# Hybrid SSD and S5 encoder layer on one core: the decayed scores go through PSUM, their differences go to ScalarE, and the norm weights are applied to four feature tiles at once

## The chip, the cores and the metric

The kernel runs on one core of one Trainium2 chip. The metric is the device time of one execution in microseconds (us), median of several runs. Every product is made in fp32r with a split operand: a value is stored as a rounded high part and a low remainder, and one product is three matmuls (high by high, high by low, low by high).

## What is computed

A layer over 2048 tokens (16 more are put ahead and dropped again), width 1024. Only the parts that matter here are shown.

```python
xn = rmsnorm(h, norm_mix_w)
z, xbc, dt_raw, u_s5, gates = split(xn @ w_in)
y_a = ssd_branch(z, xbc, dt_raw, ...)
y_b = s5_branch(u_s5, ...)
h = h + (g_a * y_a + g_b * y_b) @ w_out
h = h + square(relu(rmsnorm(h, norm_mlp_w) @ w_ff_in)) @ w_ff_out
return rmsnorm(h, final_norm_w)[16:]
...
def ssd_chunked(xs, dt, a, bm, cm):
    da_cs = cumsum(dt_c * a)
    seg = da_cs[:, :, :, None] - da_cs[:, :, None, :]
    decay = exp(where(causal, seg, -inf))
    scores = einsum("bclgn,bcsgn->bclsg", cc, bc)
    y_diag = einsum("bclsg,bclsgr,bcsgrp->bclgrp", scores, decay, xdt)
    states = einsum("bclgn,bclgr,bclgrp->bcgrpn", bc, decay_states, xdt)
    ...
    y_off = einsum("bclgn,bcgrpn,bclgr->bclgrp", cc, h_prev, exp(da_cs))
    return y_diag + y_off
```

The SSD branch has 16 heads of width 64 in 4 groups; the heads of a group share bm and cm (128 states).

## The kernel before

The work has three stages. An **initial stage** normalises all rows and makes the S5 inputs from them, while tables for S5 are set up on VectorE. Then four **mixer blocks** (b = 0 to 3) of 512 tokens follow. Last comes the **MLP**, in three row blocks; the change does not touch it.

The norm of a row tile (128 rows) is `norm_rows`: `scale_rows` multiplies 128x1024 values by a scalar of each row, `turn_rows` then transposes the eight feature tiles on TensorE into two PSUM banks of four and writes them out as high and low part with the norm weight of each feature. It runs for 16 row tiles and the 16 extra rows in the initial stage, and again for 12 row tiles (blocks 1 to 3) at the end of the block before.

A mixer block takes the groups g = 0 to 3 in turn. For a group, four tiles of the convolution's input (two of xs, one of b, one of c) and then 16 products for z and the gate run on TensorE. They are the dense work: tiles named `pd`, in four PSUM banks of their own. The SSD work rides along: after each of the group's eight weight units `step` is called, with `t` from 0 to 7, and issues some of it. It uses four other PSUM banks, which `bank` hands out in turn: a new tile waits until the tile that was four before it has been read for the last time.

Of a chunk of 128 tokens (`c` = 0 to 3), `inputs` and `front` transpose xs into the bank `sst` (L787), multiply it by dt (`xdt`, L791) and by the skip weight (`dx`, L830), make the scores in the bank `psc` (three matmuls, issued by `mm3`), mask them (`smask`, L837), multiply the decays of four heads by them (L839) and split the result (`mh` on ScalarE, L842, `ml` on VectorE, L843). `back` makes y: the part from the state (`pyo`), and for each of four heads one matmul of `mh` with both halves of `xhl` side by side (L853) and one of `ml` with the high half (L855). VectorE then adds the two halves to y one after the other (L864). `update` brings the state `hT` forward (`pS`); the next chunk's `pyo` needs it.

The decays of a group come from `decays`: a DMA on SP's queue (L885) spreads the cumulative sums `csd` over all partitions (1 MB, tile `csb`), VectorE subtracts the sum of each partition and takes the minimum with 0 (16 instructions of 128x128, L889), and ScalarE takes the exponential in place (L890). `start` is called at t = 2; `csb` has one buffer in block 0 and two in the others. `csd` of a block is written by its first step.

In block 0 the S5 recurrence also rides along (`s5.step`), with long runs of VectorE work. In what order the instructions stand on an engine is set by a scheduler when the program is built: it simulates the program and places an instruction where it thinks it ready, after the points that `tc.issue_after` names. Once built, each engine works strictly in that order.

Of the kernel before, what the change touches and what calls it, by code (L numbers as in the profile page):

```python
# [9 lines left out]
F32 = mybir.dt.float32  # L10
F32R = mybir.dt.float32r
AF = mybir.ActivationFunctionType
ALU = mybir.AluOpType
# [3 lines left out]
P = 128  # L17
# [8 lines left out]
NG = 4  # L26
# [101 lines left out]
def _body(ctx, tc, d, out):  # L128
    nc = tc.nc
    V, S, G, T = nc.vector, nc.scalar, nc.gpsimd, nc.tensor  # L130
# [14 lines left out]
    def bank(name, dt=F32):  # L145
        return pss.tile([P, 512], dt, name=name, tag="s")
# [7 lines left out]
    tri = cm.tile([P, P], F32, name="tri")  # L154
# [86 lines left out]
    def mm3(ps, lh, ll, rh, rl, first, last, open_=False):  # L241


        T.matmul(ps, lh, rh, start=first, stop=False, skip_group_check=open_)  # L244
        T.matmul(ps, lh, rl, start=False, stop=False, skip_group_check=open_)  # L245
        return T.matmul(ps, ll, rh, start=False, stop=last, skip_group_check=open_).ins  # L246
# [12 lines left out]

    def scale_rows(pl, src, L, rs):  # L260
        t = pl.tile([P, D], F32, name="nt", tag="nt", bufs=2)
        V.tensor_scalar(t[:L], src[:L], rs, None, op0=ALU.mult)
        return t

    def norm_rows(pl, src, L, rs, wcol, dh, dl, c0):
# [2 lines left out]
    def turn_rows(t, L, wcol, dh, dl, c0, qs=(0, 1)):  # L268
        for q in qs:
            p = bank("ntp")  # L270
            pv = p.rearrange("p (f l) -> p f l", f=4)[:, :, :L]
            for i in range(4):
                ft = q * 4 + i
                T.transpose(pv[:, i, :], t[:L, ft * P:(ft + 1) * P], ident[:L, :L])
            for i in range(4):
                ft = q * 4 + i
                S.activation(dh[:, ft, c0:c0 + L], pv[:, i, :], AF.Copy, scale=wcol[:, ft:ft + 1])
                V.scalar_tensor_tensor(dl[:, ft, c0:c0 + L], pv[:, i, :], wcol[:, ft:ft + 1],
                                       dh[:, ft, c0:c0 + L].bitcast(F32), op0=ALU.mult, op1=ALU.subtract)


    def s5_setup(stack):
# [493 lines left out]
    class Ssd:  # L776
# [5 lines left out]

        def inputs(self, x, dts, i0, cs_, L):
            pl = self.pl
            pt = bank("sst")
            for i in range(2):
                T.transpose(pt[:L, i * P:(i + 1) * P], self.sd.xs[:, i, cs_], ident)  # L787
            x.pth = pt[:L, 0:256].rearrange("p (h q) -> p h q", h=4)
            x.xdt = pl.tile([P, 4, 64], F32, name="xdt", tag="xdt")
            xdd = pl.tile([P, 4, 64], F32, name="xdd", tag="xdd")  # L790
            V.tensor_tensor(x.xdt[:L], x.pth, h4(dts.dt, L, i0), op=ALU.mult)  # L791
            G.tensor_tensor(xdd[:L], x.xdt[:L], h4(dts.ds, L, i0), op=ALU.mult)
            x.xddh = pl.tile([P, 256], F32R, name="xddh", tag="xddh", bufs=2)
            x.xddl = pl.tile([P, 256], F32R, name="xddl", tag="xddl", bufs=2)
            xf = xdd.rearrange("p h q -> p (h q)")
            S.copy(x.xddh[:L], xf[:L])
            G.tensor_tensor(x.xddl[:L], xf[:L], x.xddh[:L].bitcast(F32), op=ALU.subtract)
# [14 lines left out]
            G.tensor_tensor(self.hl, f, self.hh.bitcast(F32), op=ALU.subtract)  # L812

        def start(self):
            self.dec = decays(self.pl, self.dts, self.g, self.b)

        def meta_in(self):
            self.mk = _K()
# [5 lines left out]
        def front(self, c):  # L824

            pl, sd, g, x = self.pl, self.sd, self.g, self.ck[c]
            x.cs_ = cs_ = slice(sd.t0 + c * P, sd.t0 + (c + 1) * P)
            self.inputs(x, self.dts, c * NH + g * 4, cs_, P)
            x.dx = pl.tile([P, 4, 64], F32, name="dx", tag="dx", bufs=2)
            V.tensor_tensor(x.dx, x.pth, drow[:, g * 4:g * 4 + 4].unsqueeze(2).broadcast_to([P, 4, 64]), op=ALU.mult)  # L830
            x.xhl = pl.tile([P, 4, 2, 64], F32R, name="xhl", tag="xhl", bufs=2)
            S.copy(x.xhl[:, :, 0, :], x.xdt)
            G.tensor_tensor(x.xhl[:, :, 1, :], x.xdt, x.xhl[:, :, 0, :].bitcast(F32), op=ALU.subtract)
            psc = bank("psc")
            mm3(psc[:, 0:P], sd.bh[:, cs_], sd.bl[:, cs_], sd.ch[:, cs_], sd.cl[:, cs_], True, True)
            sm = pl.tile([P, P], F32, name="smask", tag="smask", bufs=2)
            V.tensor_tensor(sm, psc[:, 0:P], tri, op=ALU.mult)  # L837
            csb = self.dec[:, c]
            V.tensor_tensor(csb, csb, sm.unsqueeze(1).broadcast_to([P, 4, P]), op=ALU.mult)  # L839
            x.mh = pl.tile([P, 4, P], F32R, name="mh", tag="mh", bufs=2)  # L840
            x.ml = pl.tile([P, 4, P], F32R, name="ml", tag="ml", bufs=2)
            S.copy(x.mh, csb)  # L842
            V.tensor_tensor(x.ml, csb, x.mh.bitcast(F32), op=ALU.subtract)  # L843

        def back(self, c):

            pl, sd, g, x, dts = self.pl, self.sd, self.g, self.ck[c], self.dts
            i0, cs_ = c * NH + g * 4, x.cs_
            py, po = bank("py"), bank("pyo")
            mm3(po[:, 0:256], sd.ch[:, cs_], sd.cl[:, cs_], self.hh, self.hl, True, True)  # L850
            pyv = py.rearrange("p (h a q) -> p h a q", h=4, a=2)
            for h in range(4):
                T.matmul(pyv[:, h].rearrange("p a q -> p (a q)"), x.mh[:, h, :],  # L853
                         x.xhl[:, h].rearrange("p a q -> p (a q)"), start=True, stop=False)
                T.matmul(pyv[:, h, 0, :], x.ml[:, h, :], x.xhl[:, h, 0, :], start=False, stop=True)  # L855
            self.update(x, sd.bth[:, c, :], sd.btl[:, c, :], dts.cd, i0, P)
            if c < NC4 - 1:
                self.split()
            x.y = y = pl.tile([P, 4, 64], F32, name="y_", tag="y_", bufs=2)
            for h in range(4):  # L860
                V.scalar_tensor_tensor(y[:, h, :], po[:, h * 64:h * 64 + 64], dts.E[:, i0 + h:i0 + h + 1],
                                       x.dx[:, h, :], op0=ALU.mult, op1=ALU.add)
            for a in range(2):
                V.tensor_tensor(y, y, pyv[:, :, a, :], op=ALU.add)  # L864

        def gate(self, c):

# [13 lines left out]
    def decays(pl, dts, g, b):  # L881

        t = pl.tile([P, NC4, 4, P], F32, name="csb", tag="csb", bufs=2 if b else 1)
        src = csd[b].rearrange("(c h) l -> c h l", h=NH)[:, g * 4:g * 4 + 4, :]
        nc.sync.dma_start(t, src.unsqueeze(0).broadcast_to([P, NC4, 4, P]))  # L885
        for c in range(NC4):
            for h in range(4):
                i = c * NH + g * 4 + h
                V.tensor_scalar(t[:, c, h, :], t[:, c, h, :], dts.cs[:, i:i + 1], 0.0, op0=ALU.subtract, op1=ALU.min)  # L889
        S.activation(t, t, AF.Exp)  # L890
        return t


    xp = pool("xn", stack=xp_st)
# [195 lines left out]
    for b in range(NB):  # L1090
# [10 lines left out]
        ssd, later = {}, []  # L1101
# [11 lines left out]
        def step(mm):  # L1113

            n = step.n
            step.n += 1
            g, t = divmod(n, 8)
            with tc.issue_after(mm):
                if n == 0:
                    dts.turn()  # L1120
                    dts.sums()
                if g < NG:
                    x = ssd[g]
                    if t == 2:
                        x.start()
                    elif t == 4:
                        if b == 0:
                            x.meta_in()
                        x.front(0)
                    elif t == 5:  # L1130
                        if b == 0:
                            x.meta_out()
                        x.split()
                        x.front(1)
                    elif t == 6:
                        x.back(0)
                    elif t == 7:
                        x.front(2)
                        x.gate(0)
                if g > 0:  # L1140
                    x = ssd[g - 1]
                    if t == 0:
                        x.back(1)
                        x.gate(1)
                    elif t == 1:
                        x.front(3)
                    elif t == 2:
                        x.back(2)
                        x.gate(2)
                    elif t == 3:  # L1150
                        x.back(3)
                        x.gate(3)
                for f in later:
                    f()
                later.clear()
                if b == 0:
                    s5.step(n - 1)
                if n >= KSTART:
                    next(kept, None)
# [79 lines left out]
        for c in range(NC4):  # L1239
# [4 lines left out]
            p = bank("y5p")  # L1244
# [521 lines left out]
```

## Time and profile before

| | |
|---|---|
| median of 3 runs | 3305.94 us (3300.7 to 3306.1) |
| the profiled execution | 3306.5 us, of which 3304.8 us are the span from the first to the last instruction |
| TensorE busy | 3083.7 us, 93% |
| VectorE busy | 2105.5 us, 64% |
| ScalarE busy | 1231.2 us, 37% |
| GpSimd busy | 1428.1 us, 43% |

A group of instructions is named by its line, its engine (PE is TensorE, DVE VectorE, ACT ScalarE, POOL GpSimd, SP the queue of SyncE), and its tiles as out<-in. A busy time counts stretches in which an engine had an instruction in flight; successive instructions overlap a little, so that the busy time of a group divided by their number is less than the mean duration. An engine's idle time matters only where another engine waits for it.

### The profile page before, as it was taken

To read this page: it belongs to the slowest core of one execution; us is meant where nothing else is said; L and a number is where in the kernel's file an instruction comes from. 1 tells how busy PE (TensorE), PEld (TensorE's weight loads), DVE (VectorE), ACT (ScalarE), POOL (GpSimd) and SP (SyncE) were. 2 spreads that over 40 slices of the span, in tenths; PEclk is the share of its full clock that TensorE was granted. 3 is DMA by queue.
4 is the path that set the end of the run, shared out by engine and by line. 5 is a ranking of instruction groups with operands and counts; after the bars stand their busy time and mean duration, and the time that the engine had idled before them with its cause. 6 is when DMAs were issued, how large, how long until landed. Compare 5 with 4: busy or idle time off the path is not lost. (4 is left out here: it accounts for less than half of the span.)

```text
span 3304.8 us, 50038 instructions
## 1 busy us (share of the span) xinstructions
PE 3083.7 (93%) x18353; PEld 2751.1 (83%) x18353; DVE 2105.5 (64%) x4298; ACT 1231.2 (37%) x2573; POOL 1428.1 (43%) x1736
## 2 busy tenths in 40 slices
PE   7899999998999999998999788998979999989998
PEld 6678888877888778876888688888979999989998
DVE  8969998426843576426854477767675555475555
ACT  6345554434432443334433343344442121142222
POOL 3346766523522344213433465665642222243443
PEclk9999999999999999999999889999989999999999
DMA  6477676775556654566756767777788888889998
GB/s 210 143 214 203 199 205 205 284 245 155 173 189 216 201 169 158 204 221 195 226 178 209 255 252 275 261 275 265 276 283 284 246 250 245 249 286 377 358 358 277
DMA packets 297877, 782.92 MB, mean 237 GB/s; under 512 B 90688, under 2 KB 132800, under 8 KB 268448
## 3 DMA queue, kind: packets, MB, share of 16 engines
q0 software_dynamic: 88832, 411.21, 37.4%
q1 hardware_dynamic: 206192, 367.29, 33.8%
q8 instruction: 146, 2.39, 0.3%
q10 hardware_dynamic: 2608, 1.22, 0.1%
q14 instruction: 99, 0.81, 0.1%
HBM read 563.66 MB, written 218.05 MB: 237 GB/s over the span
## 5 line engine op out<-in xcount | busy, mean ns | idle before, releaser
L1505 DVE TENSOR_TENSOR acc<-acc,p 128x512 f32<-128x512 f32 x330 | 225.7, 684 | 171.6 <-PE p L246 169.1
L244 PE MATMUL pd<-hnh,wc 128*128 128x384 f32 (+1 forms) x896 | 292.9, 328 | 34.9 <-DMA wc<-wcd 21.3
L244 PE MATMUL pd<-wu,xnh 128*128 128x512 f32 x768 | 309.8, 404 | 3.5 <-ACT cacc L750 3.0
L246 PE MATMUL pd<-wu,xnl 128*128 128x512 f32 x768 | 308.9, 402 | 0.0
L245 PE MATMUL pd<-wu,xnh 128*128 128x512 f32 x768 | 308.3, 401 | 0.0
L246 PE MATMUL pd<-hnh,wc 128*128 128x384 f32 (+1 forms) x896 | 291.6, 328 | 13.7 <-DVE wc L1346 10.5
L245 PE MATMUL pd<-hnl,wc 128*128 128x384 f32 (+1 forms) x896 | 291.8, 326 | 0.0
L228 POOL DMA_DIRECT2D wu<-wsd x168 | 96.0, 572 | 373.0 <-PE pd L246 305.6
L1356 POOL DMA_DIRECT2D wr<-wcd x227 | 122.3, 539 | 274.8 <-PE pd L246 138.7
L244 PE MATMUL pd<-xnh,wu 128*128 128x512 f32 (+1 forms) x640 | 232.8, 364 | 7.7 <-DMA wu<-wsd 6.5
L246 PE MATMUL pd<-xnh,wu 128*128 128x512 f32 (+1 forms) x640 | 229.3, 359 | 0.0
L245 PE MATMUL pd<-xnl,wu 128*128 128x512 f32 (+1 forms) x640 | 229.0, 358 | 0.0
L1356 POOL DMA_DIRECT2D wc<-wcd x221 | 118.3, 536 | 252.8 <-PE pd L246 136.8
L244 PEld LDWEIGHTS pd<-hnh,wc 128*128 128x128 f32 x896 | 173.6, 194 | 40.0 <-ACT hnh L994 13.5
L753 DVE SCALAR_TENSOR_TENSOR cacc<-craw,conv,cacc 128x512 f32<-128x512 f32 (+1 forms) x192 | 174.9, 912 | 24.5 <-ACT cacc L750 17.1
L246 PEld LDWEIGHTS pd<-hnh,wc 128*128 128x128 f32 x896 | 173.6, 194 | 19.9 <-DVE wc L1346 14.3
L244 PEld LDWEIGHTS pd<-wu,xnh 128*128 128x128 f32 x768 | 146.1, 190 | 35.4 <-ACT cacc L750 3.9
L245 PEld LDWEIGHTS pd<-hnl,wc 128*128 128x128 f32 x896 | 173.7, 194 | 0.0
L246 PEld LDWEIGHTS pd<-wu,xnl 128*128 128x128 f32 x768 | 146.3, 191 | 31.8 <-issue 0.2
L245 PEld LDWEIGHTS pd<-wu,xnh 128*128 128x128 f32 x768 | 146.0, 190 | 31.4 <-issue 0.2
L218 POOL TENSOR_TENSOR wu<-wst,wu 128x1024 fp32r<-128x1024 f32 x56 | 137.1, 2448 | 73.6 <-ACT wu L217 72.5
L244 PEld LDWEIGHTS pd<-xnh,wu 128*128 128x128 f32 x640 | 125.5, 196 | 24.9 <-issue 7.9
(1015 smaller groups left out, 9967.7 us busy)
## 6 DMA issues: line engine op xcount, KB each, us to landing
wu<-wsd POOLq DMA_DIRECT2D x168, 1024.0 KB, 5.3
wr<-wcd POOLq DMA_DIRECT2D x227, 512.0 KB, 5.1
wcd<-wc SPq DMA_DIRECT2D x224, 512.0 KB, 3.0
wc<-wcd POOLq DMA_DIRECT2D x221, 512.0 KB, 5.5
wsd<-wu SPq DMA_DIRECT2D x56, 1024.0 KB, 5.2
wst<-in_w SPq DMA_DIRECT2D x60, 512.0 KB, 5.8
csb<-csd SPq DMA_DIRECT2D x16, 1024.0 KB, 14.3
xt<-in_x SPq DMA_DIRECT2D x28, 512.0 KB, 3.8
```

What stands on the lines that cost most here:

```text
L218: eng.tensor_tensor(t[:, 1], raw, t[:, 0].bitcast(F32), op=ALU.subtract)
L228: nc.gpsimd.dma_start(t, wsd[u - U_XBC])
L244: T.matmul(ps, lh, rh, start=first, stop=False, skip_group_check=open_)
L245: T.matmul(ps, lh, rl, start=False, stop=False, skip_group_check=open_)
L246: return T.matmul(ps, ll, rh, start=False, stop=last, skip_group_check=open_).ins
L753: V.scalar_tensor_tensor(acc[:, :n], raw[:, k:k + n], conv[:, mt, k:k + 1], acc[:, :n], op0=ALU.mult, op1=ALU.add)
L1356: nc.gpsimd.dma_start(t, wcd[di * 28 + j])
L1505: V.tensor_tensor(o, o, pv, op=ALU.add)
```

## The change

Norm: `scale_rows` runs on ScalarE. In `turn_rows` VectorE multiplies a bank of four feature tiles by its weights in place, ScalarE copies the bank out as high part, and VectorE subtracts: three instructions of 128x512 for a bank instead of eight of 128x128.

SSD: the scores go into the free columns of `sst`, the same bank that holds the transposed xs, and are masked there. The product of decays and scores goes to the bank `psc` instead of back into `csb`. The decays are made on ScalarE alone: Relu of (own sum minus spread sum), then Exp with scale -1, in two pieces at t = 2 and t = 3; the DMA is issued at the end of t = 1. For y each head takes three matmuls of 64 columns that sum in one place, so that one addition on VectorE is left.

```diff
     def scale_rows(pl, src, L, rs):
         t = pl.tile([P, D], F32, name="nt", tag="nt", bufs=2)
-        V.tensor_scalar(t[:L], src[:L], rs, None, op0=ALU.mult)
+        S.activation(t[:L], src[:L], AF.Copy, scale=rs)
         return t
...
-            for i in range(4):
-                ft = q * 4 + i
-                S.activation(dh[:, ft, c0:c0 + L], pv[:, i, :], AF.Copy, scale=wcol[:, ft:ft + 1])
-                V.scalar_tensor_tensor(dl[:, ft, c0:c0 + L], pv[:, i, :], wcol[:, ft:ft + 1],
-                                       dh[:, ft, c0:c0 + L].bitcast(F32), op0=ALU.mult, op1=ALU.subtract)
+            fs = slice(q * 4, q * 4 + 4)
+            V.tensor_tensor(pv, pv, wcol[:, fs].unsqueeze(2).broadcast_to([P, 4, L]), op=ALU.mult)
+            S.copy(dh[:, fs, c0:c0 + L], pv)
+            V.tensor_tensor(dl[:, fs, c0:c0 + L], pv, dh[:, fs, c0:c0 + L].bitcast(F32), op=ALU.subtract)
...
-            pt = bank("sst")
+            x.pt = pt = bank("sst")
...
         def start(self):
-            self.dec = decays(self.pl, self.dts, self.g, self.b)
+            self.decs = decays(self.pl, self.dts, self.g, self.b)
+            self.dec = next(self.decs)
...
-            psc = bank("psc")
-            mm3(psc[:, 0:P], sd.bh[:, cs_], sd.bl[:, cs_], sd.ch[:, cs_], sd.cl[:, cs_], True, True)
-            sm = pl.tile([P, P], F32, name="smask", tag="smask", bufs=2)
-            V.tensor_tensor(sm, psc[:, 0:P], tri, op=ALU.mult)
-            csb = self.dec[:, c]
-            V.tensor_tensor(csb, csb, sm.unsqueeze(1).broadcast_to([P, 4, P]), op=ALU.mult)
+            sm = x.pt[:, 256:256 + P]
+            mm3(sm, sd.bh[:, cs_], sd.bl[:, cs_], sd.ch[:, cs_], sd.cl[:, cs_], True, True, True)
+            V.tensor_tensor(sm, sm, tri, op=ALU.mult)
+            csb = bank("psc").rearrange("p (h l) -> p h l", h=4)
+            V.tensor_tensor(csb, self.dec[:, c], sm.unsqueeze(1).broadcast_to([P, 4, P]), op=ALU.mult)
...
-            pyv = py.rearrange("p (h a q) -> p h a q", h=4, a=2)
+            pyv = py[:, 0:256].rearrange("p (h q) -> p h q", h=4)
             for h in range(4):
-                T.matmul(pyv[:, h].rearrange("p a q -> p (a q)"), x.mh[:, h, :],
-                         x.xhl[:, h].rearrange("p a q -> p (a q)"), start=True, stop=False)
-                T.matmul(pyv[:, h, 0, :], x.ml[:, h, :], x.xhl[:, h, 0, :], start=False, stop=True)
+                mm3(pyv[:, h], x.mh[:, h, :], x.ml[:, h, :], x.xhl[:, h, 0, :], x.xhl[:, h, 1, :], True, True)
...
-            for a in range(2):
-                V.tensor_tensor(y, y, pyv[:, :, a, :], op=ALU.add)
+            V.tensor_tensor(y, y, pyv, op=ALU.add)
...
         nc.sync.dma_start(t, src.unsqueeze(0).broadcast_to([P, NC4, 4, P]))
+        yield t
         for c in range(NC4):
             for h in range(4):
                 i = c * NH + g * 4 + h
-                V.tensor_scalar(t[:, c, h, :], t[:, c, h, :], dts.cs[:, i:i + 1], 0.0, op0=ALU.subtract, op1=ALU.min)
-        S.activation(t, t, AF.Exp)
-        return t
+                S.activation(t[:, c, h, :], t[:, c, h, :], AF.Relu, bias=dts.cs[:, i:i + 1], scale=-1.0)
+            if c == 1:
+                yield
+        S.activation(t, t, AF.Exp, scale=-1.0)
+        yield
...
-                    if t == 2:
-                        x.start()
+                    if t in (2, 3):
+                        next(x.decs)
...
+                if t == 1 and g < NG:
+                    ssd[g].start()
```

The built order moves with it, at three places that the prediction speaks of. The first is TensorE in block 0, at the first chunk of group 0 (`pd` is the dense work). Before, the scores follow the transposes at once, in a bank of their own:

```order
L787 MATMUL sst_2666<-ident_72,xs_2103 128x128 x2
L245 MATMUL pd_2622<-wu_2625,xnh_1307 128x512
...
L244 MATMUL pd_2623<-wu_2625,xnh_1307 128x512
L244 MATMUL psc_2682<-ch_2106,bh_2104 128x128
L245 MATMUL psc_2682<-cl_2107,bh_2104 128x128
L246 MATMUL psc_2682<-ch_2106,bl_2105 128x128
```

Six dense matmuls stand between. After the change it is 23, and the scores go into the tile that holds the transposed xs:

```order
L786 MATMUL sst_2496<-ident_72,xs_1933 128x128 x2
L245 MATMUL pd_2451<-wu_2564,xnh_1187 128x512
...
L246 MATMUL pd_2454<-wu_2564,xnl_1188 128x512
L244 MATMUL sst_2496<-ch_1936,bh_1934 128x128
L245 MATMUL sst_2496<-cl_1937,bh_1934 128x128
L246 MATMUL sst_2496<-ch_1936,bl_1935 128x128
```

At 52 of the 64 chunks 16 or more dense matmuls stand between after the change, at seven none.

The second place is VectorE at the start of block 3 (csb_14712 is group 0's, csb_15232 group 1's). Before, both groups' subtractions stand ahead of the first product with the scores:

```order
L889 TENSOR_SCALAR csb_14712<-csb_14712,cs_14620 128x128 x16
L889 TENSOR_SCALAR csb_15232<-csb_15232,cs_14620 128x128 x16
L839 TENSOR_TENSOR csb_14712<-csb_14712,smask_14827 128x512
L839 TENSOR_TENSOR csb_14712<-csb_14712,smask_14884 128x512
L843 TENSOR_TENSOR ml_14831<-csb_14712,mh_14830 128x512
```

After the change no work on `csb` but the product with the scores is left on VectorE.

The third place is ScalarE at the same point of block 3 (csb_14479 is group 0's, csb_14990 group 1's), after the change:

```order
L886 ACTIVATE csb_14479<-csb_14479,cs_14426 128x128 x16
...
L1210 ACTIVATE zg_14789<-pd_14586 128x256
L886 ACTIVATE csb_14990<-csb_14990,cs_14426 128x128 x7
L889 ACT_TABLE_LOAD
L889 ACTIVATE csb_14479<-csb_14479 128x2048
L886 ACTIVATE csb_14990<-csb_14990,cs_14426 128x128 x9
L841 CAST mh_14635<-psc_14633 128x512
L889 ACTIVATE csb_14990<-csb_14990 128x2048
L748 COPY craw_14862<-pd_14837 128x512
```

Seven to eleven of group 1's Relus stand ahead of group 0's Exp in the blocks 1 to 3 alike, and the copies that free banks of dense work (`craw`) stand behind. On TensorE the first `py` of a block now stands 53, 61 and 49 dense matmuls later than before, in the blocks 1, 2 and 3.

## Rows read from the trace of the kernel before

**Rows 1.** Busy time by stage: length, PE, PEld, DVE, ACT, POOL (count), PEclk, DMA, GB/s
```profile
0.00:186.00 186.00, 156.47 (x822) 119.41 (x822) 157.59 (x572) 87.13 (x222) 64.59 (x78) 0.94 0.54 176
186.00:680.00 494.00, 464.88 (x2679) 396.71 (x2679) 387.38 (x752) 246.67 (x524) 308.59 (x286) 0.96 0.73 224
680.00:1810.00 1130.00, 1089.18 (x5278) 895.18 (x5277) 633.69 (x1476) 434.17 (x883) 387.23 (x608) 0.98 0.58 193
1810.00:3304.00 1494.00, 1373.15 (x9580) 1339.84 (x9578) 926.81 (x1499) 463.27 (x944) 667.68 (x766) 0.96 0.84 282
```

**Rows 2.** Waits of TensorE in block 0 (186 to 680 us): total, times, longest
```profile
PE utp L565 <- DVE s5g L592: 8.8, 2, 4.4
```

**Rows 3.** Waits of TensorE in blocks 1 to 3 (680 to 1810 us)
```profile
PE py L853 <- ACT mh L842: 16.4, 3, 10.9
...
PE sst L787 <- DVE y__11957 L861: 3.2, 1, 3.2
```

**Rows 4.** Timeline at the start of block 3: start, duration, engine, instruction, idle before
```profile
1491.52 0.93 SPq L885 DMA_DIRECT2D csb<-csd  x2
...
1505.44 3.22 DVE L889 TENSOR_SCALAR csb<-csb,cs 128x128 f32<-128x128 f32 x16 [9.73 <-DMA csb<-csd]
1512.23 3.23 DVE L889 TENSOR_SCALAR csb<-csb,cs 128x128 f32<-128x128 f32 x16 [3.57 <-DMA csb<-csd]
...
1518.05 0.45 PE L853 MATMUL py<-xhl,mh 128*128 128x128 f32 x1 [10.93 <-ACT mh L842]
```

**Rows 5.** Busy time by stretch behind the first py of blocks 1 and 3
```profile
768.00:775.00 7.00, 5.81 (x21) 5.08 (x22) 6.56 (x11) 5.03 (x8) 1.88 (x5) 0.51 0.43 152
...
1518.00:1526.00 8.00, 7.95 (x26) 6.94 (x27) 7.10 (x12) 5.08 (x11) 4.34 (x7) 0.50 0.00 1
```

**Rows 6.** Groups by line and shape, whole span: busy us, mean ns
```profile
L839 DVE TENSOR_TENSOR csb<-csb,smask 128x512 f32<-128x512 f32 x64 | 75.4, 1184 | 1.1
L278 DVE SCALAR_TENSOR_TENSOR xnl<-ntp,wmix,xnh 128x128 fp32r<-128x128 f32 x224 | 70.0, 342 | 8.3 <-ACT xnh L277 7.9
L843 DVE TENSOR_TENSOR ml<-csb,mh 128x512 fp32r<-128x512 f32 x64 | 61.1, 959 | 14.4 <-ACT mh L842 14.3
L889 DVE TENSOR_SCALAR csb<-csb,cs 128x128 f32<-128x128 f32 x256 | 56.5, 296 | 79.0 <-DMA csb<-csd 79.0
L262 DVE TENSOR_SCALAR nt<-xt,rsx 128x1024 f32<-128x1024 f32 x28 | 26.4, 941 | 9.2 <-DMA xt<-in_x 6.8 <-POOL rsx L252 1.4 <-PE ntp L274 1.0
L956 DVE TENSOR_TENSOR x<-ntp,wmlp 128x512 f32<-128x512 f32 x24 | 16.4, 684 | 4.4 <-PE ntp L955 4.3
...
L277 ACT ACTIVATE xnh<-ntp,wmix 128x128 fp32r<-128x128 f32 x224 | 72.4, 368 | 53.3 <-DVE xnl L278 44.9 <-PE ntp L274 6.0 <-DVE st L327 0.2
```

**Rows 7.** Busy time of L864 alone, blocks 0 to 3 together: DVE
```profile
sum 1624.00, DVE 53.12; mean DVE 26.56
```

**Rows 8.** Timeline of TensorE: dense work, then a chunk's y in block 3
```profile
1529.14 0.40 PE L244 MATMUL pd<-xnh,wu 128*128 128x512 f32 x1
1529.37 0.40 PE L245 MATMUL pd<-xnl,wu 128*128 128x512 f32 x1
...
1529.99 0.31 PE L853 MATMUL py<-xhl,mh 128*128 128x128 f32 x1
1530.13 0.25 PE L855 MATMUL py<-xhl,ml 128*128 128x64 f32 x1
1530.21 0.30 PE L853 MATMUL py<-xhl,mh 128*128 128x128 f32 x1
```

**Rows 9.** Timeline, first chunk of block 0: transposes on TensorE, last read on VectorE
```profile
233.49 0.38 PE L787 MATMUL sst<-ident,xs 128*128 128x128 f32 x2
...
242.39 0.41 DVE L830 TENSOR_TENSOR dx<-sst,drow 128x256 f32<-128x256 f32 x1
```

**Rows 10.** Timeline of ScalarE and VectorE at the start of block 1
```profile
756.90 0.57 ACT L749 COPY craw<-pd 128x512 f32<-128x512 f32 x1
...
762.07 1.07 DVE L889 TENSOR_SCALAR csb<-csb,cs 128x128 f32<-128x128 f32 x5 [7.02 <-DMA csb<-csd]
```

## The prediction, made before the changed kernel had run

> **What bounds the kernel.** I read the table of stages first [rows 1]. TensorE is busy 93% of the span, so the change can only give back what TensorE loses: time without a matmul, and time at the half clock. Until 1810 us it is without one for 29.5 us in the initial stage (186 - 156.5), 29.1 in block 0 and 40.8 in blocks 1 to 3. The granted clock is 0.94, 0.96 and 0.98 of full there, which is 11, 20 and 23 us of full-speed work lost. The MLP behind it, 1494 us, holds nothing that the change touches. VectorE is busy 85% of the initial stage and 78% of block 0, 56% of blocks 1 to 3; ScalarE never over 50%.
>
> Then I read what TensorE waits for. In block 0 the longest waits are for PSUM banks that VectorE has not read yet [rows 2]; nearly all others of that block name VectorE too. In blocks 1 to 3 three waits of 16.4 us together, for the first `mh` of a block, are the largest entry [rows 3]. The timeline of block 3 shows why [rows 4]: both groups' `csb` are asked for together at 1491.5; group 0's has landed at 1505.4, but VectorE then stands in front of group 1's, which lands at 1512.2, before it goes on to group 0's product. TensorE is idle for 10.93 us until 1518.05. Behind these waits it runs at half clock [rows 5]: 8 us at 0.50 in block 3 (1.2 instead of 2.4 GHz), 7 us at 0.51 in block 1.
>
> **VectorE's load.** The subtractions go (56.5 us), half of L864 (53.1 / 2 = 26.6) [rows 6, 7]. L839 and L843 get one operand in PSUM. The nearest row is L956, one PSUM operand, same shape: 16.4 / 24 = 0.68 us each instead of 75.4 / 64 = 1.18 and 61.1 / 64 = 0.96 [rows 6], so 64 x 0.50 + 64 x 0.27 = 49 us go. In all 132 us, a quarter of it (33) in block 0, of 387 there. The norm before costs 26.4 + 70.0 = 96 us; after, 56 banks x 2 x 0.68 = 77. Sixteen of 28 row tiles are in the initial stage: 11 us less of 158. Bounds: nothing gained (PSUM writing is as slow as L839 was, then L839 and L843 stay), or all of this.
>
> **ScalarE's load.** 256 Relus. The nearest row is L277, one activation of 128x128 with a scalar per partition: 72.4 / 224 = 0.32 us [rows 6], so 83 us, 5.2 a group where VectorE took 3.2 [rows 4]. In the norm 8 short activations a row tile become 2 long and the scaling, about even. ScalarE's 37% bear this; what matters is where it stands in line (below).
>
> The Trainium skill, page "ScalarE: Activation LUTs", section "Rules for kernel authors", speaks against this edit: relu, max and add belong on VectorE. On durations this trace agrees (0.32 against 0.22 us); if ScalarE were the engine waited for, that would be worth 83 - 57 = 26 us on the wrong side, and the sum below would be near zero.
>
> **TensorE.** A head's y takes 0.22 us (1529.99 to 1530.21), of which the 64-column product has 0.08 [rows 8]. Three 64-column products: 0.24, so +0.02 x 256 = +5 us. Bounds: 0, and 0.14 each (the spacing behind the 128-column product), 0.20 x 256 = +51, which I think far off since width is what tells the two apart.
>
> **Block starts (1 to 3).** TensorE's first `py` now stands 53, 61 and 49 dense matmuls later; at 0.23 us each [rows 8] that is 11 to 14 us, as long as the longest wait. VectorE no longer stands before group 1's landing; ScalarE does (7 to 11 of its Relus ahead of group 0's Exp). In block 3: group 1 landed 1512.2, 7 Relus 2.3, table and Exp 3.2, product 0.7, `mh` 0.6, some handing over: 1519.5; TensorE would come there at 1507.1 + 11.3 + 0.5 = 1519. So the 16.4 us go, and with them the clock: 7.95 x 0.5 + 5.81 x 0.49 = 6.8 us [rows 5]. Together **-23**.
>
> What is late next is the dense work's banks. In block 1 the copy of a bank at 756.9 now stands behind Relus that wait for group 1's landing (VectorE got it at 762.1 [rows 10]): Relus 3.5, table and Exp 3.2, 5 Relus 1.6 put it to 770.4, and the next bank's copies to about 779, where TensorE, two tiles of 24 x 0.23 us further, wants them at 769 and 772.5. In blocks 2 and 3 the order leaves room. **+6**, bounds 0 and 12.
>
> **The scores behind the reads.** They share a tile with the transposed xs, and are ordered behind the last read of it, `dx`. At the first chunk of block 0 that read ended 8.9 us after the transposes [rows 9]; 23 dense matmuls cover 5.3. Taking each chunk's read from the trace and its cover from the new order, the uncovered rest sums to 21 us over the 16 chunks of block 0 and 9 us over the 48 others. VectorE's lag is what the change lightens, so I take a third: **+10**, bounds 0 and 30.
>
> **Block 0** otherwise: VectorE loses 33 us in a stretch where TensorE's idle time (29) and clock loss (20) come from its lateness. I take half: **-24**; bounds 0 and -49. **Initial stage**: 11 us less on VectorE, but the first scaling is longer on ScalarE, and TensorE's first 7 us are spent waiting for that chain; I take **-4**, bounds +1 and -12.
>
> Sum: -23 + 6 + 10 + 5 - 24 - 4 = -30. The profiled execution took 3306.5 us (3304.8 of span), 0.6 above the median of the runs, so the forecast is 3306.5 - 30 - 0.5 = **3276 us**, by itself between 3250 and 3297.
>
> **Rivals.** *TensorE becomes the bound of block 0 too.* For it: its waits there name VectorE alone, and VectorE has 12% less work (33 + 13 for the products that ran longest in block 0). All bounds on the good side: -12 - 49 - 23 + 6 + 5 - 9 (the waits for `y` at `sst`, of which the longest is 3.2 [rows 3]) = -82, 3224 us. Against it: the S5 work on VectorE stays. Chance 0.15.
>
> *Scores stall TensorE*: it ends slower. One mechanism: at each chunk TensorE stands before the scores until VectorE has read `sst`, with its whole line of dense work behind. In full it is 30 us, and clock behind it in the ratio of the block starts (6.8 lost for 14.7 us of waiting), 14. With no gain in block 0 and the initial stage: 30 + 14 - 23 + 6 + 5 = +32, 3338 us. It decides from about 40 us of such loss, four times what I allow. For it: [rows 9]. Against: the scheduler left 16 or more dense matmuls at 52 chunks, and 0.8 us is enough where VectorE is free. Chance 0.13.
>
> *The wait moves to ScalarE.* All three blocks pay the 6 us that I see in one (18, with 8 of clock), VectorE's relief in block 0 brings 5, the initial stage nothing: 18 + 8 - 23 - 5 + 3 + 5 = +6, about no change, 3312 at the worst and 3300 if one block is spared. For it: both `csb` still land 7 us apart [rows 4], and the engine that stands between is now the one that frees the dense banks. The Trainium skill's rule on relu, named above, would put its weight here. Chance 0.13.
>
> **From this the numbers.** The forecast has 0.59. The range 3230 to 3312 leaves out half of the good rival and the slow one. A measurement tells about 0.2% (6.6 us) from no change. Faster by more: the forecast and the good rival, 0.73; the same: the third rival and the forecast's edge, 0.14; slower: 0.13.
>
> **What would show it.** Right: L889 gone from VectorE and Relus of about 0.3 us on ScalarE; L838 and L842 near 0.69 us each where L839 had 1.18; no wait of TensorE for `mh` at a block's start; block 0 some 17 us shorter, blocks 1 to 3 some 9 shorter, the MLP unchanged within 5 us. Wrong: waits of TensorE for `dx` at the scores over 20 us in sum, waits at `pd` for ScalarE's `cacc` at each block's start, or y products more than 0.3 us a head.

## The result and the profile after

The changed kernel takes 3412.35 us (median of 4 runs, 3410.79 to 3423.05), the kernel before 3306.02: a ratio of 1.033, 95% interval 1.031 to 1.035. That is 106 us slower, where 30 us faster was forecast; it lies outside the range and beyond the slow rival (3338).

The first view is the busy time by stage of the changed kernel, columns as in [rows 1]; the stages end about where TensorE has issued as many dense matmuls as at the ends of the stages before (exactly there the initial stage ends at 176.8 us, the others at 708.6 and 1916.3).

```profile
0.00:179.00 179.00, 149.98 (x832) 117.49 (x833) 150.40 (x487) 82.40 (x137) 63.49 (x78) 0.98 0.57 184
179.00:709.00 530.00, 488.43 (x2734) 419.19 (x2733) 343.82 (x653) 264.82 (x568) 293.02 (x286) 0.92 0.69 209
709.00:1916.00 1207.00, 1131.47 (x5466) 924.38 (x5466) 556.30 (x1196) 480.64 (x1035) 360.00 (x608) 0.97 0.54 181
1916.00:3409.00 1493.00, 1368.38 (x9582) 1336.02 (x9580) 926.48 (x1500) 463.49 (x944) 670.24 (x766) 0.97 0.84 282
```

Against [rows 1], with the exact ends: the initial stage ends 9 us earlier, block 0 is 38 us longer (532 for 494), blocks 1 to 3 are 78 longer (1208 for 1130), the MLP is unchanged (1493 for 1494). Until the MLP, VectorE is 128 us less busy, of the 151 that were counted (132 and the norm's 19), and it did not help. Adding up, for the time until the MLP, the gaps between matmuls and half of the matmul time at the lower clock, in both traces: idle time of TensorE rose from 92 to 135 us, clock loss from 39 to 63, and the rest, which is matmul time at full speed, from 1672 to 1707. The narrow products of y account for most of this last rise: made alone, they add 25 us of matmul time.

Next the waits of TensorE in block 0 (first two rows) and in blocks 1 to 3 (the others): total, times, longest.

```profile
PE sst L244 <- DVE dx L830: 9.4, 4, 5.0
PE pyo L244 <- ACT hTh L810: 8.6, 4, 5.2
...
PE pd L244 <- ACT zg L1210: 18.4, 9, 6.6
PE pyo L244 <- ACT hTh L810: 13.2, 5, 7.7
PE sst L244 <- DVE dx L830: 6.3, 4, 3.5
```

The 16.4 us for `mh` [rows 3] are gone. In their place stand waits for the split of the state (`hTh`), for copies on ScalarE that free dense banks (`zg`), and at the scores for `dx`, 15.7 us in all. These are spread thin; no one of them is the 106 us. The longest stretch without dense work shows no great wait at all. It is the end of block 0, first dense work alone, then TensorE as a whole (length, PE busy, PEclk, DMA, GB/s):

```profile
498.50:548.50 50.00, 24.38 (x85) 0.83 0.56 125
548.50:597.50 49.00, 0.05 (x1) 0.67 0.42 126
...
548.50:597.50 49.00, 39.82 (x199) 0.67 0.42 126
```

For 49.3 us (548.5 to 597.9) TensorE does no dense work; in the kernel before, the longest such stretch of block 0 is 6.0 us. It is busy for 39.8 of 49 us with SSD and S5 work, without cover for the chains between, at a clock of 0.67. The dense work of the block was used up early (at the 258th high-by-high matmul of the block's dense work TensorE is 52 us earlier than before), and the last four chunks came after it: in the trace all dense matmuls of the block's groups have gone when chunk 12 makes its scores; before, only chunk 15 was near that.

This stretch is a sign and not the whole bill. Most of the loss lies in blocks 1 to 3, where no stretch without dense work is longer than 14 us (15 before): there the idle time of TensorE rose by 35 us in all, its clock loss by 11 and its matmul time by 32. And e14 below, in which 90 of the 93 us of the scores part are gone, still has such a stretch of 34 us at the end of block 0. Why the chunks are late is what the experiments are about.

### The profile page after: what moved, and what is told of

It reads as the page before. It is cut to its first block, busy times and chain, and to the rows that moved or that the text cites. A ratio compares the mean times of both kernels' runs of the same rounds, so it can differ in the third digit from the quotient of the medians.

```text
span 3409.1 us, 50343 instructions
## 1 busy us (share of the span) xinstructions
PE 3138.3 (92%) x18609; PEld 2797.1 (82%) x18609; DVE 1977.0 (58%) x3833; ACT 1291.4 (38%) x2684; POOL 1386.8 (41%) x1736
```

## The experiments

Each gives the ratio to the kernel before on the same chip, with its 95% interval. The change has four parts that can be made alone: norm, scores (shared tile and product in PSUM), decays (on ScalarE, DMA a step earlier) and y (three narrow products, one addition). The first eight runs make each alone and leave each out. Three theories stood against each other: that the narrow products of y cost the time (P), that the scores part does (S), or that work given to ScalarE does (A).

**y.**

```diff
-T.matmul(... x.mh[:, h, :], x.xhl[:, h] both halves ...); T.matmul(... x.ml ...)
+mm3(pyv[:, h], x.mh[:, h, :], x.ml[:, h, :], x.xhl[:, h, 0, :], x.xhl[:, h, 1, :], True, True)
```

> The kernel before with the three 64-column products and the single addition for y, and nothing else of the change. Theory P (narrow products): in the trace after the change a chunk's 12 products took 1.255 us where 8 took 0.81, so 64 chunks cost 28.5 us more; alone this edit should cost 20 to 45 us (3326 to 3350), the single addition giving back little, since VectorE is not waited for in blocks 1 to 3. Theory S (scores) and theory A (ScalarE): about no change, 3300 to 3312, the extra products being covered by waits that are there anyway.

> The whole change but for y, which keeps its two products a head and its two additions. Theory P: the slowdown of 106 us falls by 30 to 60 (to 3350 to 3380), clock included. Theories S and A: it falls by less than 15 (3397 to 3412).

Alone 1.0063 (1.0047 to 1.0079), 21 us; leaving it out of the change brings 4 us (1.0318, 1.0303 to 1.0334). So theory P holds for y by itself and explains 4 of the 106. Without y's edit the matmul time until the MLP is 27 us shorter, but idle time and clock loss are 23 us longer. The price is in the timeline of the changed kernel:

```profile
560.92 0.19 PE L244 MATMUL py<-xhl,mh 128*128 128x64 f32 x1
560.95 0.27 PE L245 MATMUL py<-xhl,mh 128*128 128x64 f32 x1
561.06 0.28 PE L246 MATMUL py<-xhl,ml 128*128 128x64 f32 x1
561.17 0.28 PE L244 MATMUL py<-xhl,mh 128*128 128x64 f32 x1
```

One starts every 0.11 us although it is 64 columns wide, as long as the 128-column products had on average (0.22 / 2, [rows 8]): what is paid is the new 128x128 weight tile of each, not the width. The weight loads of both kernels start 0.11 us apart here, behind 128 columns as behind 64. Twelve take 1.255 us where eight took 0.81, 28.5 us over 64 chunks. The Trainium skill, page "TensorE: Matmul & The Clock Gate", section "LDWEIGHTS (loading the stationary operand)", gives columns / 1.2 ns for such a load, by which one of 128 columns would be estimated at 107 ns. The trace agrees: the loads and the products start 110 to 112 ns apart at the full clock (a load's own row, which overlaps the next, is 190 ns long).

**Scores.**

```diff
+sm = x.pt[:, 256:256 + P]   # scores beside the transposed xs
+csb = bank("psc").rearrange("p (h l) -> p h l", h=4)   # product in PSUM
```

> The kernel before with the scores in the tile of the transposed xs and the product with the decays in PSUM, and nothing else. Theory S: scores ordered behind the last read of that tile and a fourth bank held longer push SSD work later and leave it without dense work at a block's end: 30 to 60 us slower (3336 to 3366). Theory P and theory A: faster by 5 to 25 (3281 to 3301), since L839 and L843 get shorter.

> The whole change but for the scores, which keep a bank of their own and a product in SBUF. Theory S: the slowdown falls by 40 to 70 us (3342 to 3372), and the waits of TensorE at sst for dx are gone. Theory P and theory A: it stays within 20 us of the change (3392 to 3432).

Alone 1.0283 (1.0266 to 1.0300), 93 us; the change without it 1.0067 (1.0051 to 1.0084), 22 us. This is the part, and it is larger than theory S said on both sides (30 to 60 alone, 40 to 70 in the change, where it is 87).

**Decays.**

```diff
-V.tensor_scalar(t[:, c, h, :], t[:, c, h, :], dts.cs[:, i:i + 1], 0.0, op0=ALU.subtract, op1=ALU.min)
+S.activation(t[:, c, h, :], t[:, c, h, :], AF.Relu, bias=dts.cs[:, i:i + 1], scale=-1.0)
... (the two pieces, the Exp and the earlier DMA as in the change)
```

> The kernel before with the decays on ScalarE alone (Relu, then Exp, two pieces, DMA issued at the end of t = 1), and nothing else. Theory A (ScalarE): Relus and Exp stand ahead of the copies that free dense banks and of the split of the state; TensorE waits for zg and hTh as in the trace after the change (18.4 + 13.2 us in blocks 1 to 3): 15 to 40 us slower (3321 to 3346). Theory P and theory S: the waits for the first mh go (16.4 us and 6.8 of clock): 10 to 25 faster (3281 to 3296).

> The whole change but for the decays, which stay with VectorE's subtraction and minimum and start at t = 2. Theory A: the slowdown falls by 30 to 60 us (3352 to 3382). Theory P and theory S: the waits for the first mh come back, so within 5 us of the change or up to 25 slower than it (3407 to 3437).

Alone 1.0019 (1.0006 to 1.0031), 4 us; leaving it out brings 22 (1.0262, 1.0247 to 1.0278). Both times between the two theories: the waits for `mh` do fall, and others come. Waits of TensorE from 680 to 1830 us with the decays alone:

```profile
PE psc L244 <- ACT ch L759: 11.3, 5, 4.4
...
PE btp L767 <- ACT cacc L758: 8.7, 3, 4.9
PE pd L244 <- ACT zg L1215: 7.8, 2, 7.1
PE py L854 <- ACT mh L843: 5.1, 3, 3.0
```

16.4 has become 5.1, but 27.8 us are now spent on work of ScalarE (`ch`, `cacc`, `zg`); before, `ch` had 3.5 and `cacc` 3.0. In the five longest of these waits, 24 us together, ScalarE is at Relus and exponentials for nearly all of the time. The rule of the Trainium skill that the prediction weighed (page "ScalarE: Activation LUTs", "Rules for kernel authors") came out right here, by 4 and 22 us. The waits show work that stands in line behind the Relus; what their mere length costs was not tried apart.

**Norm.**

```diff
-V.tensor_scalar(t[:L], src[:L], rs, None, op0=ALU.mult)
+S.activation(t[:L], src[:L], AF.Copy, scale=rs)
... (and the three instructions of a bank in turn_rows, as in the change)
```

> The kernel before with the norm's weights applied to four feature tiles at once and its scaling on ScalarE, and nothing else. By the trace after the change the initial stage ended 9 us earlier: 5 to 15 us faster (3291 to 3301) by all theories, unless the scaling on ScalarE at the end of blocks 0 to 2 delays the banks there (then no change).

> The whole change but for the norm. If the norm's part is worth its 9 us in the initial stage: 5 to 15 us slower than the change (3417 to 3427). If the scaling and the copies on ScalarE at the end of the blocks are part of the 40 us that blocks 1 to 3 lose in their later two thirds (theory A): faster than the change, 3370 to 3400.

Alone 0.9966 (0.9955 to 0.9977), 11 us faster; leaving it out costs 6 (1.0348, 1.0331 to 1.0366). The initial stage is 9 us shorter with it. As expected.

The single parts, -11 + 93 + 4 + 21 = 107 us, add up to the 106, but y and the decays are worth something else in the change (4 and 22) than alone, so that the sum is partly chance.

**The halves of the scores part.** The next runs take it apart: only the product in PSUM (in the bank that held the scores), only the shared tile, and the whole part with the scores issued ahead of the reads.

```diff
 # e9: scores in their own bank, smask in SBUF
+csb = psc.rearrange("p (h l) -> p h l", h=4)
 # e10: shared tile, product in place in SBUF as before
+sm = x.pt[:, 256:256 + P]
 csb = self.dec[:, c]
 # e11: in inputs(), right behind the transposes
+mm3(pt[:, 256:256 + P], sd.bh[:, cs_], sd.bl[:, cs_], sd.ch[:, cs_], sd.cl[:, cs_], True, True, True)
```

> The kernel before with the product of decays and scores written to PSUM, into the bank that held the scores; scores keep that bank, smask stays in SBUF. Theory O (order: what costs is that the scores stand behind the reads of the shared tile, 25 to 28 dense matmuls behind the transposes instead of 10 to 12): transposes to smask stays at 3 to 4 us, and the run is 0 to 25 us faster than before (3279 to 3304), by the 49 us that L839 and L843 lose on VectorE. Theory B (bank: the full bank psc, held until ml has been made, makes the turn of the four banks slower): 30 to 90 us slower than before (3334 to 3394).

> The kernel before with the scores in the tile of the transposed xs, masked there; the product stays in SBUF, in csb. Theory O: as slow as the whole scores part, 60 to 100 us over before (3364 to 3404), transposes to smask at 6 to 8 us. Theory B: within 15 us of before (3289 to 3319).

> The scores part of the change, with one thing different: the three matmuls of the scores are issued right behind the transposes, ahead of the two reads of the shared tile (xdt, dx). Theory O: the scores wait for nothing on VectorE, transposes to smask falls back to 4 us or less, and the 93 us go, all but 20 (3285 to 3325). Theory B: still 60 us or more slower than before (over 3364).

> The kernel before with the norm of the change and the product in PSUM in the scores' own bank; y, decays and the place of the scores as before. Theory O: the norm's 11 us and what the product brings, 3270 to 3293, the fastest of all. Theory B: over 3320.

e9: 0.9987 (0.9976 to 0.9999). e10: 0.9977 (0.9963 to 0.9990). e11: 1.0059 (1.0044 to 1.0074), so 74 of the 93 us are gone. e12: 1.0010 (0.9995 to 1.0024), a miss: the 11 us of the norm don't show beside the product in PSUM; its block 0 is 502 us long where the two edits alone had 493 and 489. Theory O fell with e10: there the scores stand as late as in the change, 8.4 us from transposes to mask, and it costs nothing. Theory B said so of e10, but fell with e9, where the full bank is held until `ml` has been made and costs nothing either, and with e11. Neither half is harmful; the two together are.

What they do together shows in VectorE's and TensorE's rows of the changed kernel for two successive chunks of block 1: transposes, last read, scores, mask, product, `ml`, and only then the next chunk's transposes.

```profile
853.58 0.63 PE L786 MATMUL sst<-ident,xs 128*128 128x128 f32 x2
...
856.49 0.41 DVE L830 TENSOR_TENSOR dx<-sst,drow 128x256 f32<-128x256 f32 x1
...
862.27 0.22 PE L244 MATMUL sst<-ch,bh 128*128 128x128 f32 x1
...
864.40 0.29 DVE L836 TENSOR_TENSOR sst<-sst,tri 128x128 f32<-128x128 f32 x1
...
865.26 0.69 DVE L838 TENSOR_TENSOR psc<-csb,sst 128x512 f32<-128x512 f32 x1
...
866.60 0.69 DVE L842 TENSOR_TENSOR ml<-psc,mh 128x512 fp32r<-128x512 f32 x1
...
868.80 0.38 PE L786 MATMUL sst<-ident,xs 128*128 128x128 f32 x2
```

The two chunks start 15 us apart. In the kernel before, the same two chunks' transposes start 3.7 us apart (first and second row; the scores shown are the second chunk's), and the first product is behind both:

```profile
806.46 0.66 PE L787 MATMUL sst<-ident,xs 128*128 128x128 f32 x2 [3.08 <-DVE y__8595 L861]
...
810.11 0.63 PE L787 MATMUL sst<-ident,xs 128*128 128x128 f32 x2
810.39 0.46 PE L244 MATMUL psc<-ch,bh 128*128 128x128 f32 x1
...
814.31 1.23 DVE L839 TENSOR_TENSOR csb<-csb,smask 128x512 f32<-128x512 f32 x1
```

Over all 16 groups, the time from the first chunk's transposes to the second's, and from a chunk's second transpose to its mask (means from the traces), and, in the built order of group 0 of block 1, the dense matmuls between the transposes of chunks 0 and 1:

| run | transposes, chunk 0 to 1 | transposes to mask | dense between chunks 0 and 1 | ratio |
|---|---|---|---|---|
| before | 7.0 us | 3.5 us | 12 | 1 |
| e9, product in PSUM | 6.3 | 3.1 | 12 | 0.9987 |
| e10, shared tile | 6.1 | 8.4 | 6 | 0.9977 |
| e11, scores first | 11.2 | 4.2 | 84 | 1.0059 |
| e3, whole scores part | 13.8 | 7.2 | 84 | 1.0283 |
| the change | 16.9 | 6.9 | 122 | 1.0330 |

So the chunks tend to be serial, one chain behind the other, where the product asks for a bank of its own: the second chunk's transposes start behind the first one's product in 13 of 16 groups of the change and in 10 of e3, against 7 before and 2 in e10. In e9 `psc` is first written by the scores, early. In e3 and e11 it is first written by the product, which needs the decays and the masked scores; and the next chunk's `sst`, asked for behind it, is ordered behind it. A long link (scores behind the reads) times a serial chain makes the 93 us: e10 has the long link alone and costs nothing, e11 the serial chain with a short one and costs 19.

**Which request does it.** Two theories for the serial chain: the queue of requests just told (Q), or the turn of the four banks (R): with five requests a chunk, `pS` takes the bank that the next chunk's `sst` holds until its product.

```diff
 # e13: the change, with
-py, po = bank("py"), bank("pyo")
+py = bank("py")
+po = py[:, 256:512]
 # e14 (scores part) and e16 (the change), ahead of dx
+csb = bank("psc").rearrange("p (h l) -> p h l", h=4)
+V.memset(csb[:, 0, 0:1], 0.0)
```

> The whole change, with y's sums and the part from the state in one bank: four requests of banks a chunk instead of five, so that pS no longer takes the bank that the next chunk's sst holds. Theory R (the banks' turn: the state waits for the next chunk's product through the bank): 50 to 85 of the 106 us go (3327 to 3362). Theory Q (queue of requests: the transposes of a chunk, which ask for a bank behind the product of the chunk before, are ordered behind that product): at most 20 us go (3392 to 3420), since the built order still puts chunk 1's transposes 110 to 120 dense matmuls later than before.

> The scores part of the change (3396 alone) with the bank psc asked for ahead of dx and one element of it set to 0 there by VectorE, so that the bank is taken early; scores still in the tile of the transposed xs and behind its reads, product still in PSUM, five banks a chunk in the same turn. Theory Q: the next chunk's transposes come early again, and 55 to 90 of the 93 us go (3306 to 3341). Theory R: at most 25 us go (over 3371).

> The whole change with psc asked for and one element set ahead of dx. Theory Q: 55 to 90 of the 106 us go (3322 to 3357), and what is left is the narrow products of y. Theory R: at most 25 go (over 3387).

e13: 1.0325 (1.0300 to 1.0350), as slow as the change, with the first two chunks 18.2 us apart: R falls. e14: 1.0010 (0.9997 to 1.0024), so one instruction of 59 ns a chunk takes 90 of the 93 us away; e16: 1.0074 (1.0051 to 1.0096), 85 of 106. In e14 the mask is still 7.5 us behind the transposes, but the chunks go 4.9 us apart. The same two chunks in e14:

```profile
811.52 0.41 PE L787 MATMUL sst<-ident,xs 128*128 128x128 f32 x2
...
812.04 0.06 DVE L830 MEMSET psc<- 128x1 f32 x1
...
814.27 0.41 PE L787 MATMUL sst<-ident,xs 128*128 128x128 f32 x2 [1.17 <-DVE y__8595 L864]
...
815.06 0.06 DVE L830 MEMSET psc<- 128x1 f32 x1
...
818.64 0.22 PE L244 MATMUL sst<-ch,bh 128*128 128x128 f32 x1
```

The second transposes stand ahead of the first chunk's scores again. That taking `psc` early is the cure is shown (its request moved ahead of `dx` together with its first write; which of the two does it was not tried apart). That the scheduler hands out banks in the order of the requests is inferred from it and from the built orders.

**What is left, and a better kernel.**

> The norm of the change and the scores in the tile of the transposed xs, product in csb as before, y and decays as before. By the single edits (-11 and -8): 3277 to 3292; if the order of block 0 that the scheduler finds is as unlucky as with the norm and the product together, about 3300.

> The whole change with psc asked for and one element set ahead of dx, and y as before (two products a head, two additions). If theory Q and the narrow products are all that makes the change slow, the 20 us that e16 still lost go: 3293 to 3310. If something else in the change costs as much, 3315 or more.

> e17 without the decays on ScalarE: norm, scores part with psc taken early, y and decays as before. If the decays on ScalarE are what e17 still loses (they stand there ahead of the copies of the dense banks): 3288 to 3303. If it is the norm together with the scores part (its scaling and copies on ScalarE at the blocks' ends, the order in block 0): 3312 or more.

e15, norm and shared tile (diffs above), is 0.9956 (0.9939 to 0.9973), 15 us faster than before and the lowest of all versions; its interval overlaps that of the norm alone, and its profiled execution has 14 us of the gain in the MLP, which the edits do not touch. Until the MLP it is 9 us shorter than before, where the norm alone is 12 shorter, so that it is not shown to be better than the norm alone. e17 is 1.0092 (1.0075 to 1.0109), 29 us over: the narrow products are not what e16 had left, a miss. e18, without the decays too, is still 1.0061 (1.0041 to 1.0081). So some 20 us come from norm and scores part side by side, though alone they have -11 and (with the early write) +3. Against e14, the profiled execution of e18 has 10 us more in block 0, and 12 more in the MLP, which neither edit touches and whose length differs by up to 18 us between the profiles of these versions. This is not settled.

## Why the prediction was wrong

**The scores behind the reads (+10, bounds 0 and 30)** is the step that failed: +93 alone, +87 in the change. It priced only how long TensorE might stand at the scores. In the change that size was about right, 15.7 us of waits for `dx` at the scores, below the 20 that the prediction had named as a sign of being wrong; with the scores part alone they are 30.5, its upper bound. e10 shows that late scores by themselves are free: there the waits are 3.7. What the step left out is the other half of the same edit: the bank `psc` changed its first writer from TensorE's scores to VectorE's product. That moved the next chunk's transposes, and it could have been read in the built order: 122 dense matmuls between the first two chunks' transposes in group 0 of block 1 instead of 12. The prediction looked at the distance from transposes to scores only, took the dense work between for cover, and did not ask where the next chunk's transposes would stand. The rival *scores stall TensorE* had the place and the side, not the mechanism: its 30 us of stall and 14 of clock are half of what the part costs, and with `psc` taken early (e14) the scores are as late and 90 of the 93 us are gone.

**Block starts (-23)**: the waits for `mh` went in the change, as said, and fell to 5.1 us with the decays alone, but there 27.8 us of waits for ScalarE took their place, and the time was 4 us over. The dense banks (+6) were the right worry, and `ch` and `cacc` belonged beside them. This is the rival *the wait moves to ScalarE*.

**Block 0 (-24)**: half of the 49 us that TensorE loses there was taken as gained. (The 20 us of clock in it are 16, counted over the matmuls alone.) With the product in PSUM alone (e9) VectorE is 18 us less busy in block 0 (369 for 387 [rows 1]) and the block 5 us shorter (489 for 494), a quarter of it. Without the scores part of the change (e4) VectorE's relief is about as large and the block 4 us shorter, though the narrow products of y, which are in it too, add 6 us of matmul time. In the change, where VectorE has 44 us less, nothing came back. TensorE's waits name VectorE; that this is because chains of work go through it, which are not shorter by what it does elsewhere, fits these numbers but was not tried.

**y (+5, bounds 0 and 51)**: 21 alone. The 0.08 us of [rows 8] is the spacing behind one product and its 0.14 that behind the other; their mean, 0.11, was the price of a matmul with new weights, and the row gave it. A head's three products take 1.255 / 4 = 0.31 us, over the 0.3 that the prediction had named as a sign of being wrong. In the change y costs 4, since without it most of its time comes back as idle time and clock loss.

**Initial stage (-4)**: 9 shorter with the norm alone, within its bounds. The durations on VectorE were right: L838 and L842 at 0.69 us, which by themselves bring little (the product in PSUM 4 us, the shared tile 8).

## What to carry to other kernels

A tile of a rotating pool counts from its request, and here the built order put a later request behind the first write of an earlier one. When an edit gives a bank to a late result, look in the built order at where the next round's first instruction stands, and at how much independent work is left to cover it, not only at the wait beside the edit. If the bank is needed, write it early. Work taken off an engine that is not the bound bought little here (5 us of block 0 for 18 us of VectorE), and work given to one that frees buffers brought waits of its own (27.8 us).

## What the runs showed of the hardware

A multiplication of 128x512 fp32 values on VectorE took 682 to 697 ns for all 64 instances with one input in PSUM, the output in PSUM. Minimum, median and maximum of the line, first the change, then e9, where both inputs are in SBUF and the output in PSUM, then before, all in SBUF:

```profile
L838 DVE TENSOR_TENSOR psc<-csb,sst x64: 682/695/697, 239.6 to 1827.0; 128x512 f32<-128x512 f32 x64
```

```profile
L839 DVE TENSOR_TENSOR psc<-csb,smask x64: 684/924/2260, 244.8 to 1696.3; 128x512 f32<-128x512 f32 x64
```

```profile
L839 DVE TENSOR_TENSOR csb<-csb,smask x64: 677/1004/2657, 242.7 to 1704.6; 128x512 f32<-128x512 f32 x64
```

It is the input in PSUM that takes the spread away; where the output lies hardly matters. e10, with that input and the output in SBUF, has 653 to 689. What the slower instances wait for was not tried.
